# Down projection of the FFN: 14 of 22 row tiles by seven products instead of 12, one output block's plain products moved into the second phase, and ScalarE's table loaded early

## Chip, cores and metric

The kernel runs as one program on one core of a Trainium2 chip. The metric is the device time of one execution in microseconds, and lower is better. PE is TensorE, DVE is VectorE, ACT is ScalarE, SP issues the DMAs.

## What is computed

Two decoder layers run on a sequence of 512 tokens with a width of 1024. Each layer is a half-step FFN, a mixer of three branches, and a second half-step FFN, and each of these ends in a residual sum and a layer norm. So there are four FFNs, and they are what the change touches:

```
def swiglu(x, w_gate, w_up, w_down):
    return (jax.nn.silu(x @ w_gate) * (x @ w_up)) @ w_down

h = layer_norm(DEEPNORM_ALPHA * h + 0.5 * swiglu(h, ffn1_w_gate[l], ffn1_w_up[l], ffn1_w_down[l]), ln1_g[l], ln1_b[l])
mix = hybrid_mixer(h, cos, sin, ...)
h = layer_norm(DEEPNORM_ALPHA * h + mix, ln2_g[l], ln2_b[l])
h = layer_norm(DEEPNORM_ALPHA * h + 0.5 * swiglu(h, ffn2_w_gate[l], ffn2_w_up[l], ffn2_w_down[l]), ln3_g[l], ln3_b[l])
```

`x` is 512 x 1024, `w_gate` and `w_up` are 1024 x 2816, and `w_down` is 2816 x 1024. Everything is float32.

## The kernel before

**Splitting.** A float32 product is made of three fp32r matmuls (`mm3`): high by high, high by low, low by high. So each operand has to be split first. ACT casts the high part (`S.copy(h, src)`), and DVE subtracts it to get the low part (`split_into`). Every 512 columns of weight or of hidden feature thus cost one ACT and one DVE instruction before PE can use them.

**Down projection.** `token_out` computes the down product with tokens as output rows: four token tiles `tt` of 128 rows, two column halves `hf` of 512. Each (tt, hf) is one PSUM bank, and there are eight banks. The inner dimension has 22 row tiles of 128 (`NF`). The first `2 * DOWN_FAST` of them go through `seven_out`, the rest are plain products.

**Seven products.** `seven_out` takes row tile f with row tile g = f + n, and cuts the problem into a 2 x 2 block product: token halves (tiles 0 and 1, tiles 2 and 3), row tiles (f, g), column halves. It uses a seven-product scheme in place of the eight block products. Its three phases loop over all pairs: phase 1 makes two products per pair (banks `x` and `y`), phase 2 three (`v`, `x`, `y`), phase 3 two (`z`, `v`). A product is two token tiles by three matmuls of 512 columns, so 6 matmuls. Between the phases DVE adds what a bank holds so far to the residual (`norm.add`). Phase sums of operands (`t1`, `t3`, `t2`, `t4`, and those of the hidden features) are made on DVE.

**Plain row tiles.** After `seven_out`, the other row tiles are taken two at a time (a "plain pair", one weight block of 256 rows by 512 columns from `load`): first for hf 0 and all four token tiles, where `prepare` also splits the two hidden features, then for hf 1. In the second half `TAIL = 5` holds all five blocks at once, so that the token tiles end one after the other. Each is then normalised (`norm.half`, `norm.finish`), written out and transposed into the next stage's input (`to_features`).

**Order.** Nothing runs in the order written. A `Planner` records every instruction with an estimated cost, gives it a due time (PE's clock at the point where it was recorded, plus a bias), and lays all engines' queues out by a list schedule before the program is built. Buffers bound how far an engine may run ahead: 76 slots of 128 x 512 (`N_SLOTS`), of which 28 for streamed weights (`WEIGHTS`), 5 raw weight buffers (`RAWS`), 8 PSUM banks.

**Tables.** `rope_setup` runs beside the first FFN's down projection with a bias of 60 us. It uses ACT's Sin. The mixer's first special function after it is the Exp in `params`.

Of the kernel before, what the change touches and what calls it, by code (L numbers as in the profile page):

```python
# [13 lines left out]
AF = mybir.ActivationFunctionType  # L14
# [5 lines left out]
NT = T // 128  # L20
KD = D // 128
FF = 2816
NF = FF // 128
# [5 lines left out]
ALPHA = (2 * DEPTH) ** 0.25  # L29
# [265 lines left out]
FIRST_BIAS = 0.1  # L295
SECOND_BIAS = 0.6
SUM_BIAS = 6.0
TAIL = 5
DOWN_FAST = 6
TAIL_OUT = 4  # L300
WINDOW = 150.0
KEEP_LATER = 3.0
# [45 lines left out]
def trunk(tc, a, out):  # L348
    pl = Planner(tc)

    with ExitStack() as ctx:
# [12 lines left out]
        def bank(name="ps"):  # L364
            return pl.tile(ps_p, [128, 512], F32, "ps", 8)

        def small(shape, name, bufs=None):
            return pl.tile(tiny, shape, F32, name, bufs or 2)
# [177 lines left out]
                    to_features(tt, self.then == "mixer")  # L546

        LO, HI = slice(0, 256), slice(256, 512)

        def token_out(norm, wsrc, n, ah, al, tail, prepare=None, a32=None, fast=0):  # L550


            def load(hf, fp, hold=False):
                return wblock(wsrc[fp * 256:(fp + 1) * 256, hf * 512:(hf + 1) * 512], hold)

            def acc(ps, tt, f, w, j, first, more):
                c = slice(tt * 128, (tt + 1) * 128)
                mm3(ps, ah[f][:, c], al[f][:, c], w[0][j], w[1][j], first, f == n - 1, more)

            banks = seven_out(norm, wsrc, a32, fast) if fast else {}  # L560
            norm.load()
            for hf in range(2):
                ps = [banks.get((tt, hf)) or bank("dn") for tt in range(NT)]
                old = [(tt, hf) in banks for tt in range(NT)]
                rest = tail if hf else 0
                for fp in range(fast, n // 2 - rest):
                    w = load(hf, fp)
                    for j in range(2):
                        if prepare and not hf:
                            prepare(2 * fp + j)  # L570
                        for tt in range(NT):
                            acc(ps[tt], tt, 2 * fp + j, w, j, fp + j == fast and not old[tt], old[tt])
                ws = [load(hf, fp, True) for fp in range(n // 2 - rest, n // 2)]
                for tt in range(NT):
                    for i, w in enumerate(ws):
                        for j in range(2):
                            f = n - 2 * rest + 2 * i + j
                            acc(ps[tt], tt, f, w, j, f == 2 * fast and not old[tt], old[tt])
                    norm.half(tt, hf, ps[tt])
                    if hf:  # L580
                        norm.finish(tt)

        def seven_out(norm, wsrc, a32, n):
            pairs = [(i, n + i) for i in range(n)]

            def rows(f, cols=slice(0, D)):
                m = cols.stop - cols.start
                raw = pl.tile(wraw_p, [128, m], F32, "raw", RAWS)
                Q.dma_start(out=raw, in_=wsrc[f * 128:(f + 1) * 128, cols])
                return [raw[:, c:c + 512] for c in range(0, m, 512)]  # L590

            def wsplit(w):
                h, lo = slot(F32R, WEIGHTS), slot(F32R, WEIGHTS)
                split_into(h, lo, w)
                return h, lo

            def halves(op, c):
                return op[0][:, c], op[1][:, c]

            def product(to, op, w, i, more=False):  # L600
                for t in range(2):
                    c = slice(t * 128, (t + 1) * 128)
                    mm3(to[t], op[0][:, c], op[1][:, c], w[0], w[1], i == 0 and not more, i == n - 1, more)

            two = lambda: [bank("dn") for _ in range(2)]
            x, y = two(), two()
            s23, t2 = [], []
            for i, (f, g) in enumerate(pairs):
                b11, b12 = rows(f)
                s = slot()  # L610
                s23.append(s)
                V.tensor_tensor(s[:, HI], a32[f][:, LO], a32[f][:, HI], op=SUB)
                V.tensor_tensor(a32[f][:, HI], a32[f][:, HI], a32[g][:, HI], op=ADD)
                op = split(a32[f])
                t1 = slot(F32, WEIGHTS)
                V.tensor_tensor(t1, b12, b11, op=SUB)
                product(x, halves(op, LO), wsplit(b11), i)
                product(y, halves(op, HI), wsplit(t1), i)
            for t in range(2):
                norm.add(t, 0, x[t])  # L620
                norm.add(2 + t, 1, y[t])
            v = two()
            for i, (f, g) in enumerate(pairs):
                (b11, b12), (b22,) = rows(f), rows(g, slice(512, 1024))
                s = s23[i]
                V.tensor_tensor(s[:, LO], a32[f][:, HI], a32[f][:, LO], op=SUB)
                V.tensor_tensor(a32[f][:, LO], a32[g][:, LO], s[:, LO], op=SUB)
                op = split(s)
                s4 = slot(F32R)
                s4 = s4[:, LO], s4[:, HI]  # L630
                split_into(*s4, a32[f][:, LO])
                t3 = slot(F32, WEIGHTS)
                t2.append(slot())
                V.tensor_tensor(t3, b22, b12, op=SUB)
                V.tensor_tensor(t2[i], t3, b11, op=ADD)
                product(v, halves(op, HI), wsplit(t3), i)
                product(x, halves(op, LO), wsplit(t2[i]), i, True)
                product(y, s4, wsplit(b22), i, True)
            for t in range(2):
                norm.add(2 + t, 1, v[t])  # L640
                norm.add(t, 1, x[t])
                norm.add(2 + t, 0, x[t])
                norm.add(2 + t, 1, x[t])
            z = two()
            for i, (f, g) in enumerate(pairs):
                b21, = rows(g, slice(0, 512))
                op = split(a32[g])
                t4 = slot(F32, WEIGHTS)
                V.tensor_tensor(t4, b21, t2[i], op=SUB)
                product(z, halves(op, LO), wsplit(b21), i)  # L650
                product(v, halves(op, HI), wsplit(t4), i, True)
            return {(0, 0): z[0], (1, 0): z[1], (2, 0): v[0], (3, 0): v[1], (0, 1): y[0], (1, 1): y[1]}

# [89 lines left out]
        def ffn(l, wg, wu, wd, g, b, src, then, beside=None):  # L745
# [40 lines left out]
                with pl.stream(bias=60.0):  # L786
                    beside()
            residual(src)
            token_out(Norm(g[l], b[l], 4 * ALPHA, 16 * EPS, then), wd, NF, hh, hl, TAIL, prepare, hid, DOWN_FAST)


        def rope_setup():
# [22 lines left out]
            V.scalar_tensor_tensor(ang, ang, -1.0, ang, op0=MUL, op1=MAX)  # L815
            V.tensor_scalar(ang, ang, -1.0, float(np.float32(np.pi / 2)), op0=MUL, op1=ADD)
            S.activation(cos, ang, AF.Sin)
            Q.dma_start(out=trig[:, 0], in_=cos)
            Q.dma_start(out=trig[:, 1], in_=sin)

# [585 lines left out]
```

## Time and profile before

| what | value |
|---|---|
| median of 3 runs | 2413.03 us (2411.71 to 2415.16) |
| time of the profiled execution | 2411.15 us |
| its span from first to last instruction | 2409.4 us |
| granted TensorE clock over the span | 0.999 |
| busy: PE, DVE, ACT | 2384.3, 2219.6, 1332.8 us |

The profiled execution's own time is 1.75 us over its span, and 1.9 us under the median. Busy time is the union of an engine's instruction records. Matmul and vector records overlap the next one's, so the distance from start to start in a dense run tells more of the cost than a record's length does. All instructions carry line L288, which is the planner's issuing loop, so groups are told apart by tiles and shapes: `s` is any slot, `raw` a weight as it came from memory, `ps` a PSUM bank, `xh` and `xl` the split features.

### The profile page before, as it was taken

What the parts mean: (1) busy time and instruction counts of PE and PEld (TensorE: products, weight loads), DVE (VectorE), ACT (ScalarE), POOL (GpSimd) and SP (SyncE); (2) the same over time, 40 slices, a digit from 0 to 9 for tenths busy, and PEclk for the clock granted to TensorE, in tenths of its full rate; (3) what the DMA queues carried; (4) which work ended last, traced back from release to release, by engine and by line L of the source; (5) the groups of instructions that cost most, each with busy time, mean ns of one, the idle gap of its engine ahead of it and who ended that gap; (6) DMA issues with size and microseconds to landing.
All of it is one profiled execution on the core that took longest, in us unless ns stands there. A gap on an engine that the chain in (4) does not pass through costs nothing.

```text
span 2409.4 us, 41697 instructions
## 1 busy us (share of the span) xinstructions
PE 2384.3 (99%) x15812; PEld 2185.5 (91%) x15812; DVE 2219.6 (92%) x4567; ACT 1332.8 (55%) x2863; POOL 0.2 (0%) x4
## 2 busy tenths in 40 slices
PE   9999999999999999999999999999999999999998
PEld 8999888889899899998899998888889998999986
DVE  8998987999999799989799999789999997999996
ACT  6555538536756445656356565294376563555560
POOL 0000000000000000000000000000000000000000
PEclk9999999999999999999999999999999999999999
DMA  5334562322233623334523345523123335233451
GB/s 168 106 110 154 160 183 71 104 55 74 78 107 97 210 71 106 105 115 158 183 88 106 105 157 173 167 58 99 43 74 97 105 106 184 88 106 106 148 162 67
DMA packets 269834, 280.34 MB, mean 116 GB/s; under 512 B 18676, under 2 KB 221632, under 8 KB 269632
## 3 DMA queue, kind: packets, MB, share of 16 engines
q1 hardware_dynamic: 269632, 277.67, 38.3%
q8 instruction: 124, 2.03, 0.3%
q14 instruction: 78, 0.64, 0.1%
HBM read 260.33 MB, written 17.30 MB: 115 GB/s over the span
## 4 chain that ended last, share of the span: by engine, by line
PE 90%; DVE 5%; ACT 3%; DMA 1%; issue 1%; SPq 0%; DVEq 0%; ACTq 0%
PE ps L288 90%; DVE s L288 4%; ACT s L288 2%; ACT ps L288 1%; DMA raw<-in_w_out 0%; DMA raw<-in_w_in 0%; ACT xh L288 0%; DMA s<-in_x 0%; DVE lny L288 0%; DVE lnt L288 0%; DVE xl L288 0%; DMA xspill<-s 0%; DMA s<-in_cv_dw_b 0%; SPq L288 0%; DVE mx L288 0%
## 5 line engine op out<-in xcount | busy, mean ns | idle before, releaser
L288 PE MATMUL ps<-s 128*128 128x256 f32 (+2 forms) x9164 | 1516.3, 321 | 2.8 <-ACT s L288 1.9
L288 PEld LDWEIGHTS ps<-s 128*128 128x128 f32 x9164 | 1331.7, 190 | 133.6 <-ACT s L288 4.7
L288 PE MATMUL ps<-xh,s 128*128 128x256 f32 (+2 forms) x4064 | 901.4, 307 | 1.2 <-ACT s L288 1.2
L288 DVE TENSOR_TENSOR s<-s 128x512 fp32r<-128x512 f32 (+8 forms) x1264 | 718.3, 601 | 6.5 <-ACT s L288 4.2
L288 PEld LDWEIGHTS ps<-xh,s 128*128 128x128 f32 (+1 forms) x4064 | 678.7, 190 | 34.3 <-ACT s L288 1.6
L288 PE MATMUL ps<-xl,s 128*128 128x256 f32 (+2 forms) x2032 | 624.6, 308 | 0.0
L288 ACT CAST s<-raw 128x512 fp32r<-128x512 f32 (+1 forms) x716 | 424.1, 620 | 258.1 <-DMA raw<-in_ffn_w_down 67.7
L288 DVE TENSOR_TENSOR s<-raw,s 128x512 fp32r<-128x512 f32 (+1 forms) x844 | 549.3, 680 | 12.6 <-ACT s L288 10.9
L288 ACT CAST s<-s 128x512 fp32r<-128x512 f32 (+2 forms) x796 | 441.7, 591 | 165.6 <-DVE s L288 157.1
L288 ACT COPY s<-ps 128x256 f32<-128x256 f32 (+4 forms) x616 | 254.9, 419 | 349.6 <-PE ps L288 347.4
L288 PEld LDWEIGHTS ps<-xl,s 128*128 128x128 f32 (+1 forms) x2032 | 386.9, 190 | 16.7 <-DVE xl L288 0.2
L288 DVE SCALAR_TENSOR_TENSOR s<-s 128x512 f32<-128x512 f32 (+26 forms) x356 | 250.3, 714 | 2.9 <-ACT s L288 2.6
L288 DVE TENSOR_TENSOR s<-ps,s 128x256 f32<-128x256 f32 (+1 forms) x336 | 147.0, 438 | 62.8 <-PE ps L288 51.7
L288 DVE TENSOR_TENSOR s<-raw 128x512 f32<-128x512 f32 x256 | 172.9, 682 | 5.3 <-DMA raw<-in_ffn_w_gate 3.8
L288 ACT ACTIVATE s<-s 128x512 f32<-128x512 f32 x162 | 102.5, 667 | 51.5 <-DVE s L288 49.1
L288 PE MATMUL ps<-ident,s 128*128 128x128 f32 (+1 forms) x508 | 86.9, 278 | 11.8 <-DMA s<-in_x 4.5
L288 ACT CAST xh<-ps 128x512 fp32r<-128x512 f32 x48 | 28.6, 596 | 124.3 <-PE ps L288 124.3
L288 DVE TENSOR_TENSOR s<-s,raw 128x512 f32<-128x512 f32 x128 | 87.2, 681 | 0.0
L288 PEld LDWEIGHTS ps<-ident,s 128*128 128x128 f32 (+1 forms) x508 | 61.1, 142 | 28.5 <-issue 11.1
L288 DVE TENSOR_TENSOR s<-s,ps 128x512 f32<-128x512 f32 x76 | 50.5, 680 | 30.1 <-PE ps L288 30.0
L288 DVE SCALAR_TENSOR_TENSOR s<-s,ps 128x512 f32<-128x512 f32 x96 | 63.2, 679 | 15.9 <-PE ps L288 14.5
L288 DVE SCALAR_TENSOR_TENSOR s<-ps,s 128x510 f32<-128x510 f32 (+3 forms) x88 | 64.4, 740 | 0.1
(100 smaller groups left out, 573.5 us busy)
## 6 DMA issues: line engine op xcount, KB each, us to landing
raw<-in_w_in SPq DMA_DIRECT2D x106, 512.0 KB, 3.8
raw<-in_ffn_w_down SPq DMA_DIRECT2D x88, 512.0 KB, 4.4
raw<-in_ffn_w_gate SPq DMA_DIRECT2D x80, 512.0 KB, 3.8
raw<-in_ffn_w_up SPq DMA_DIRECT2D x80, 512.0 KB, 3.8
raw<-in_ffn_w_down SPq DMA_DIRECT2D x48, 256.0 KB, 2.6
spill<-s SPq DMA_DIRECT2D x40, 256.0 KB, 2.0
s<-spill SPq DMA_DIRECT2D x40, 256.0 KB, 4.2
raw<-in_w_out SPq DMA_DIRECT2D x16, 512.0 KB, 4.4
```

The costliest lines, as they stand in the source:

```text
L288: self.issued = o["f"](*o["a"], **o["k"])
```

## The change

`DOWN_FAST` goes from 6 to 7: seven pairs of row tiles go by seven products, and four plain pairs are left instead of five. In `seven_out` the roles of the two token halves are swapped (`LO`, `HI`, and the banks that go with them), so that the block which `seven_out` finishes by itself is token tiles 0 and 1 of hf 1, instead of tiles 2 and 3. For that block the plain products go to two banks of their own (`mine`), and they are made inside phase 2: `ahead()` is called after pairs 1, 2, 3, ... of phase 2 and makes one plain pair each time, with its `prepare`. After `seven_out` the plain weights of hf 0 are all held (`ws`), those of hf 1 are loaded and split a second time (`ws2`) for token tiles 2 and 3, and the token tiles end one after the other. In `rope_setup` a Tanh of one column is added behind the second Sin.

```diff
-TAIL = 5
-DOWN_FAST = 6
+AHEAD_AT = 1
+DOWN_FAST = 7
...
-            banks = seven_out(norm, wsrc, a32, fast) if fast else {}
+            banks = {}
+            if fast:
+                mine = [bank("dn") for _ in FIRST]
+                pairs = iter(range(fast, n // 2))
+
+                def ahead():
+
+                    for fp in pairs:
+                        w = load(1, fp)
+                        for j in range(2):
+                            prepare(2 * fp + j)
+                            for tt in FIRST:
+                                acc(mine[tt], tt, 2 * fp + j, w, j, fp + j == fast, False)
+                        return
+                banks = seven_out(norm, wsrc, a32, fast, ahead)
             norm.load()
+            if fast:
+                for fp in pairs:
+                    raise ValueError("pairs left")
+                ws = [load(0, fp, True) for fp in range(fast, n // 2)]
+                ws2 = []
+                for tt in range(NT):
+                    if tt in SECOND and not ws2:
+                        ws2 = [load(1, fp, True) for fp in range(fast, n // 2)]
+                    for hf, w2 in enumerate((ws, ws2)):
+                        ps = mine[tt] if hf and tt in FIRST else banks[tt, hf]
+                        if ps not in mine:
+                            for i, w in enumerate(w2):
+                                for j in range(2):
+                                    acc(ps, tt, 2 * fast + 2 * i + j, w, j, False, True)
+                        norm.half(tt, hf, ps)
+                    norm.finish(tt)
+                return
...
-        def seven_out(norm, wsrc, a32, n):
+        def seven_out(norm, wsrc, a32, n, ahead):
+            LO, HI = slice(256, 512), slice(0, 256)
...
+                if i >= n + AHEAD_AT:
+                    ahead()
             for t in range(2):
-                norm.add(t, 0, x[t])
-                norm.add(2 + t, 1, y[t])
+                norm.add(2 + t, 0, x[t])
+                norm.add(t, 1, y[t])
...
+                if i >= AHEAD_AT:
+                    ahead()
             for t in range(2):
-                norm.add(2 + t, 1, v[t])
+                norm.add(t, 1, v[t])
+                norm.add(2 + t, 1, x[t])
+                norm.add(t, 0, x[t])
                 norm.add(t, 1, x[t])
-                norm.add(2 + t, 0, x[t])
-                norm.add(2 + t, 1, x[t])
+            for _ in pairs:
+                ahead()
...
-            return {(0, 0): z[0], (1, 0): z[1], (2, 0): v[0], (3, 0): v[1], (0, 1): y[0], (1, 1): y[1]}
+            return {(2, 0): z[0], (3, 0): z[1], (0, 0): v[0], (1, 0): v[1], (2, 1): y[0], (3, 1): y[1]}
...
-            token_out(Norm(g[l], b[l], 4 * ALPHA, 16 * EPS, then), wd, NF, hh, hl, TAIL, prepare, hid, DOWN_FAST)
+            token_out(Norm(g[l], b[l], 4 * ALPHA, 16 * EPS, then), wd, NF, hh, hl, 0, prepare, hid, DOWN_FAST)
...
             S.activation(cos, ang, AF.Sin)
+
+            S.activation(small([128, 1], "one"), cos[:, 0:1], AF.Tanh)
```

## Rows read from the trace of the kernel before

**Rows 1.** The page: the span, the busy time of PE, its weight loads, DVE and ACT, and the chain of work that ended last by engine.
```profile
span 2409.4 us, 41697 instructions
PE 2384.3 (99%) x15812; PEld 2185.5 (91%) x15812; DVE 2219.6 (92%) x4567; ACT 1332.8 (55%) x2863; POOL 0.2 (0%) x4
PE 90%; DVE 5%; ACT 3%; DMA 1%; issue 1%; SPq 0%; DVEq 0%; ACTq 0%
```

**Rows 2.** The chain that ended last, in order of time (start us, us, what): a piece in the first FFN's down projection, the long pieces that hold the other three, and the pieces behind the last matmul.
```profile
272.69 10.30 DVE s L288 x17
...
864.29 349.42 PE ps L288 x2459
...
1221.62 321.37 PE ps L288 x2260
...
2058.09 342.12 PE ps L288 x2398
2400.23 0.70 DVE s L288
...
2405.65 0.66 DVEq L1402
```

**Rows 3.** Busy time of each engine in the four stretches of the down projection, from its first products to the last matmul of the plain part (stretch: us, then busy us and instructions of PE, weight loads, DVE, ACT, GpSimd, then granted clock, DMA share, GB/s).
```profile
237.50:352.60 115.10, 114.31 (x520) 94.63 (x519) 105.94 (x205) 59.43 (x108) 0.00 (x0) 1.00 0.57 170
1093.80:1208.10 114.30, 114.30 (x522) 94.88 (x521) 101.87 (x192) 57.17 (x105) 0.00 (x0) 1.00 0.49 155
1434.60:1549.00 114.40, 114.40 (x524) 95.14 (x524) 101.93 (x200) 54.90 (x103) 0.00 (x0) 1.00 0.56 165
2288.50:2400.20 111.70, 111.69 (x498) 92.20 (x496) 93.72 (x181) 43.29 (x80) 0.00 (x0) 1.00 0.37 117
```

**Rows 4.** The same columns for the stretch behind each of the first three: the start of the mixer, of the next FFN, and of the second mixer.
```profile
352.60:375.00 22.40, 20.42 (x170) 19.89 (x169) 16.34 (x43) 8.91 (x18) 0.00 (x0) 1.00 0.63 190
1208.10:1231.00 22.90, 22.77 (x187) 22.13 (x187) 22.46 (x58) 12.18 (x29) 0.00 (x0) 1.00 0.20 69
1549.00:1571.00 22.00, 21.35 (x174) 20.50 (x173) 15.65 (x39) 9.20 (x18) 0.00 (x0) 1.00 0.62 192
```

**Rows 5.** PE's timeline (start us, us, instruction, count) inside the second FFN's down projection: two unbroken runs of 512-column matmuls.
```profile
1103.69 20.56 PE L288 MATMUL ps<-s 128*128 128x512 f32 x90
...
1123.64 26.68 PE L288 MATMUL ps<-s 128*128 128x512 f32 x117
```

**Rows 6.** DVE's timeline in the same stretch: a run of twelve low-part subtractions of 512 columns, a run of one of 256 columns and one of 512, and the three longest idle times near its end (idle us and what ended it in brackets).
```profile
1160.33 7.30 DVE L288 TENSOR_TENSOR s<-raw,s 128x512 fp32r<-128x512 f32 x12
...
1119.83 1.01 DVE L288 TENSOR_TENSOR s<-s 128x256 f32<-128x256 f32 x2
...
1172.46 1.90 DVE L288 TENSOR_TENSOR s<-raw,s 128x512 fp32r<-128x512 f32 x3 [2.26 <-ACT s L288]
1177.11 1.37 DVE L288 TENSOR_TENSOR s<-s,ps 128x512 f32<-128x512 f32 x2 [2.75 <-PE ps L288]
...
1185.95 0.69 DVE L288 TENSOR_TENSOR s<-s,ps 128x512 f32<-128x512 f32 x1 [3.89 <-PE ps L288]
```

**Rows 7.** DVE's groups in that stretch by shape (count, busy us, mean ns of one record, idle before): the low parts of weights.
```profile
L288 DVE TENSOR_TENSOR s<-raw,s 128x512 fp32r<-128x512 f32 x44 | 28.5, 682 | 2.7 <-ACT s L288 2.6
```

**Rows 8.** DVE's timeline in that stretch: the eight additions of bank contents to the residual at the end of phase 2.
```profile
1132.35 1.27 DVE L288 TENSOR_TENSOR s<-s,ps 128x512 f32<-128x512 f32 x2
1133.59 1.28 DVE L288 SCALAR_TENSOR_TENSOR s<-s,ps 128x512 f32<-128x512 f32 x2
1134.79 0.68 DVE L288 TENSOR_TENSOR s<-s,ps 128x512 f32<-128x512 f32 x1
1135.39 1.28 DVE L288 SCALAR_TENSOR_TENSOR s<-s,ps 128x512 f32<-128x512 f32 x2
1136.58 0.68 DVE L288 TENSOR_TENSOR s<-s,ps 128x512 f32<-128x512 f32 x1
```

**Rows 9.** PE's timeline in the first FFN's down projection, where it waited (idle us and what ended it in brackets).
```profile
283.03 3.26 PE L288 MATMUL ps<-s 128*128 128x512 f32 x13 [0.79 <-DVE s L288]
```

**Rows 10.** PE's timeline behind the down projections of the first and the third FFN: the transposes of token tiles 2 and 3 into the mixer's input, with the wait before them.
```profile
355.31 0.63 PE L288 MATMUL ps<-ident,s 128*128 128x128 f32 x4 [1.74 <-DVE s L288]
...
362.79 0.63 PE L288 MATMUL ps<-ident,s 128*128 128x128 f32 x4 [0.24 <-DVE s L288]
...
1550.27 0.63 PE L288 MATMUL ps<-ident,s 128*128 128x128 f32 x4 [0.31 <-DVE s L288]
...
1557.74 0.63 PE L288 MATMUL ps<-ident,s 128*128 128x128 f32 x4 [0.23 <-DVE s L288]
```

**Rows 11.** DVE's timeline at the same two places: the second low part of token tile 1's features, with its wait.
```profile
349.10 0.69 DVE L288 TENSOR_TENSOR xl<-ps,xh 128x512 fp32r<-128x512 f32 x1 [1.68 <-ACT s L288]
...
1544.05 0.69 DVE L288 TENSOR_TENSOR xl<-ps,xh 128x512 fp32r<-128x512 f32 x1 [0.26 <-ACT s L288]
```

**Rows 12.** ACT's timeline: from the load of Sin's table to the work behind the second Sin, and from the cast before the next table load to the Exp behind it.
```profile
304.67 1.28 ACT L288 ACT_TABLE_LOAD   x1
...
308.75 0.63 ACT L288 ACTIVATE s<-s 128x512 f32<-128x512 f32 x1 [1.12 <-DVE s L288]
312.57 1.14 ACT L288 CAST s<-raw 128x512 fp32r<-128x512 f32 x2 [3.18 <-DMA raw<-in_ffn_w_down]
...
346.47 0.61 ACT L288 CAST xh<-ps 128x512 fp32r<-128x512 f32 x1
347.09 1.28 ACT L288 ACT_TABLE_LOAD   x1
348.39 0.20 ACT L288 ACTIVATE sc<-sc 128x4 f32<-128x4 f32 x1
```

**Rows 13.** The page's DMA issues of the down weights (count, KB each, median us to landing), and the DMA columns (last two) of two stretches near the end of the second FFN's down projection.
```profile
raw<-in_ffn_w_down SPq DMA_DIRECT2D x88, 512.0 KB, 4.4
raw<-in_ffn_w_down SPq DMA_DIRECT2D x48, 256.0 KB, 2.6
...
1150.00:1160.00 10.00, 10.00 (x46) 8.29 (x45) 10.00 (x18) 4.91 (x9) 0.00 (x0) 1.00 0.97 315
1160.00:1170.00 10.00, 10.00 (x46) 8.29 (x45) 9.52 (x16) 6.21 (x11) 0.00 (x0) 1.00 0.86 254
```

More of the change, by code (lines that the diff above doesn't have):

```diff
@@ L548, in trunk @@
         LO, HI = slice(0, 256), slice(256, 512)
+        FIRST, SECOND = (0, 1), (2, 3)
         def token_out(norm, wsrc, n, ah, al, tail, prepare=None, a32=None, fast=0):
@@ L568, in token_out @@
                     for j in range(2):
-                        if prepare and not hf:
-                            prepare(2 * fp + j)
                         for tt in range(NT):
```

## The prediction

> **What bounds the kernel now.** I read the page first. PE is busy for 2384.3 of 2409.4 us, DVE for 2219.6, and 90% of the chain that ended last is PE [rows 1]. So time is won by taking matmuls out, as long as DVE (92%) keeps up. Then the chain in order of time: the down projections of the second, third and fourth FFN lie in unbroken pieces of PE of 349, 321 and 342 us; only the first FFN's has a piece of DVE in it, 10.3 us long [rows 2]. The stretches say how much room DVE has there: it is idle for 115.1 - 105.9 = 9.2 us in the first down projection, 12.4 in the second, 12.5 in the third, 18.0 in the fourth [rows 3]. Behind the second there is next to none (22.9 - 22.46 = 0.4), in the mixers some 6 us [rows 4].
>
> **Matmuls taken out.** A seven-product pair takes 7 x 6 = 42 matmuls of 512 columns, two plain row tiles 2 x 8 x 3 = 48. One pair more saves 6 of 492 per FFN, 24 in all. In dense runs such matmuls start (20.56 - 0.39) / 89 = 0.2266 us apart, 0.39 being about the length of the last record, and the second run gives the same [rows 5]. Gain: 24 x 0.2266 = 5.44 us if PE never waits more than now. The stage goes from 111.5 to 110.1 us. Moving the plain products of one block changes no count.
>
> **Work added to DVE.** Back to back, DVE's 512-column instructions start (7.30 - 0.68) / 11 = 0.602 us apart, and a 256-column one takes 1.01 - 0.68 = 0.33 [rows 6]. By the code a pair in phase 1 needs 4 long and 2 short instructions (3.07 us, beside 2.72 of PE), in phase 2 six and three (4.60, beside 4.08), in phase 3 four (2.41, beside 2.72): 10.1 us in all. Two plain row tiles needed six (3.6 us). On top, the hf 1 weights of the four plain pairs are now split twice, which adds 4 x 2 x 0.602 = 4.8. Sum: 10.1 - 3.6 + 4.8 = +11.3 us per FFN. ACT gains less than 8 us of its own beside 50 us of idle time in the stage [rows 3], so it is costed at nothing.
>
> Does this fit? Two accounts. First the peak inside `seven_out`: DVE's work from the stage's start minus PE's. Before: 6 x 10.1 + 12 additions x 0.602 = 67.8 against 42 x 6 x 0.2266 = 57.1, so DVE must be 10.7 us ahead when the stage starts, and it is, since PE does not wait in three of the four stages [rows 2]. After: 7 x 10.1 + 7.2 + four calls of `ahead` at 2.41 = 87.5 against (294 + 48) x 0.2266 = 77.5, so 10.0 us. The moved products bring as much PE work as DVE work (12 matmuls, 2.72 us, against 2.41) and pay for the seventh pair. The test in phase 1 is never true (i stops at 6), and phase 2 has calls enough for all four pairs. So no new stall here. Then the whole stage: DVE needs 11.3 us more in 1.4 us less. That leaves 18.0 - 12.7 = 5.3 us in the fourth stage, -0.2 and -0.3 in the third and second, -3.5 in the first. The third's lack has 6 us of room behind it, the second's only 0.4 [rows 4]. The first's falls into a stretch with room, though one where PE waits on chains of DVE and ACT. I take 1 us of new PE wait for the first and 0.5 for the second: +1.5. The bounds are 0 (work of low due time slides into idle time) and +22 (each of the three tight stages can use only half of its idle time, 6 us: three times that plus what does not fit). I lean to the low end since three stages show no wait of PE today.
>
> **Banks.** Phase 2 now holds all eight banks (`x`, `y`, `v`, `mine`), so `z` has to wait until DVE has read `x`. Before, two were spare. The eight reads take 4.9 us [rows 8]. The first `z` bank needs three reads of an `x` that is complete one product (1.36 us) before the phase ends, so it is free about half a us late, and the first two `v` products of phase 3 (2.7 us) can go in between. Bounds: 0, and 4.9 - 2.7 = 2.2 us per stage. I take 0, because the list schedule may reorder and DVE has the operands early.
>
> **Memory.** Each FFN loads 4 blocks of 512 KB and 2 of 256 KB more, 2.5 MB. The end of the stage moved 250 to 315 GB/s already [rows 13]; `ws` and `ws2` together are 4 MB for 33 us, 127 GB/s, with the next stage's weights behind them on SP's queue. Hidden; if the cover is gone, one late block costs its 4.4 us. The 16 slots of `ws2` also take room from the next stage's first weights until token tile 3 has used `ws`.
>
> **The table.** Sin's table is followed today by a second load at 347.1, between two features of token tile 1, and the Exp behind it starts 1.30 us later [rows 12]. DVE waits 1.68 us there for ACT, and 0.26 in the second mixer, which needs no load [rows 11]; PE then waits 1.74 us for token tile 2 in the first, 0.31 in the second [rows 10]. So the load costs PE 1.43 us. With the Tanh it moves right behind the Sin, where ACT idles for 3.18 us until a weight lands [rows 12]: -1.43 (bounds: 0, if it lands on another wait, and -1.74). The Trainium skill, "ScalarE: Activation LUTs", What ACT_TABLE_LOAD costs, gives a drain of about 1380 ns beside the 1283 ns of the load, 2.66 us in all. By that page the sum would be 1.2 us lower; the trace does not show that drain.
>
> **The end of the stage.** Token tiles 0, 1 and 2 now end 27.2, 21.8 and 10.9 us before the last matmul (the last two take 48 matmuls each); today all four are 30 matmuls, 6.8 us, apart. Their norms no longer queue up in DVE, so what is left of the waits for tiles 2 and 3 (0.31 + 0.31 + 0.24 + 0.23 [rows 10]) should shrink: -0.6, bounds 0 and -1.1. The end of the kernel stays: DVE starts with the last matmul there and needs the same chain [rows 2]. The wait of 0.79 us in the first FFN [rows 9] comes from `rope_setup`, which still falls into phase 2 or 3; it stays.
>
> **Sum.** -5.44 - 1.43 - 0.6 + 1.5 = -6.0 us. Against the profiled execution's 2411.15 that is 2405.2; the median of the runs is 1.9 higher, so 2407.0.
>
> **Rivals.**
> - The gain is eaten: every stage loses 1.5 us of PE, to the `z` banks or to a late split. -5.44 - 2.0 + 6 = -1.4, so 2411.6. For it: eight banks of eight, and DVE without idle time. Against: PE finds other products to do.
> - DVE becomes the bound, ending slower. The place is the plain part, where `ws2` and the norms of tiles 0 and 1 fall due together. If half of the idle time is unusable, the three tight stages lose 22 us: 2413.0 - 7.5 + 22 = 2427.5. It decides for slower once new waits pass 12.3 us, some 3 to 4 per stage. For it: negative room in three stages. Against: DVE's idle times of 2.3, 2.8 and 3.9 us near the end were waits for lack of work [rows 6].
> - No overlap on DVE. Records of these instructions are 0.682 us long [rows 7], against 0.602 from start to start. If the added ones took their whole length, each FFN would gain 16 x 0.682 + 5 x 0.42 = 13.0 us of DVE, and lack 5.2, 2.0 and 1.9 us in the first three: -7.5 + 9.1 = +1.6, 2414.6. The Trainium skill, "VectorE: DVE Perf Modes", The DRAIN you can't avoid, says that the next instruction waits until the pipe is empty, and would have it so. The twelve in 7.30 us contradict it [rows 6].
> - More is won: no new wait, and the waits of rows 9 and 10 all go: -5.44 - 2.5 - 0.8 = -8.7, 2404.3 [rows 9, 10].
> - The table part does nothing, because the mixer's start waits on something else: -5.44 - 0.6 + 1.5 = -4.5, 2408.5.
>
> **How the numbers follow.** Chances: forecast 0.52 (2404 to 2409.5), gain eaten 0.22, DVE bound 0.10, more won 0.08, no table gain 0.05, no overlap 0.03. A measurement can tell 0.2%, 4.8 us, from no change, so faster means below 2408.2. Of the forecast 0.45 lies there, with 0.08 of "more" and 0.03 of "no table gain": 0.56. The rest of these (0.07 and 0.02), with 0.22 and 0.03, makes 0.34 within. Slower is 0.10. The range, 2403 to 2413.5, takes in the forecast, "more" and most of "gain eaten", and leaves out "DVE bound", "no overlap" and the edges.
>
> **What would show it.** 24 matmuls fewer; DVE busy some 45 us more; in the down stretches no wait of PE over 1 us; no table load near the first mixer's start, and the wait of 1.74 us gone. It is wrong if PE shows waits on DVE in phase 3 or the plain part, or on a bank at the start of phase 3, or if the next FFN's first products wait for their weights.

## The result, and the profile after

The changed kernel takes 2427.94 us (median of four runs, 2425.19 to 2428.19) against 2413.7 for the kernel before beside it: a ratio of 1.0059, interval 1.0047 to 1.0071. It is slower by 14.2 us where 6.0 less was forecast, and it lies outside the range. The profiled execution took 2427.96 us, 1.9 over its span.

The page of the changed kernel, answering [rows 1]: the span, busy time and instructions by engine, the bytes moved, and the chain that ended last by engine.

```profile
span 2426.1 us, 41864 instructions
PE 2391.0 (99%) x15788; PEld 2184.1 (90%) x15788; DVE 2262.0 (93%) x4651; ACT 1360.2 (56%) x2916; POOL 0.2 (0%) x4
DMA packets 274314, 290.82 MB, mean 120 GB/s; under 512 B 19060, under 2 KB 222016, under 8 KB 274112
PE 81%; DVE 10%; DMA 4%; ACT 3%; issue 1%; DVEq 0%; SPq 0%; ACTq 0%
```

The counts are as forecast: 24 matmuls fewer, and DVE busy 42.4 us more, with 84 instructions more. The chain is 81% PE where it was 90%, and DVE has 10% of it; such shares point at DVE but settle nothing, for the chain of e13 below, a kernel faster than before, has 81% and 12%.

To see where the time went I cut both traces at the first and the last 512-column matmul of the unbroken run that makes up each down projection and each mixer's output product (us, worked out from the traces, good to some 0.4; `up` is the rest of an FFN, `mix` all of a mixer ahead of its output product; the output products are alike and left out):

| | up 1 | down 1 | mix 1 | up 2 | down 2 | up 3 | down 3 | mix 2 | up 4 | down 4 |
|---|---|---|---|---|---|---|---|---|---|---|
| before | 239.2 | 113.1 | 465.0 | 228.6 | 112.0 | 229.0 | 111.8 | 462.4 | 228.6 | 110.1 |
| after | 240.8 | 123.6 | 466.1 | 228.6 | 113.0 | 228.4 | 112.6 | 462.3 | 231.5 | 109.6 |

The first down projection loses 10.5 us. The second and third lose 1.0 and 0.8 instead of gaining 1.4. Of the four only the last, with no stage behind it, gains (0.5). The two profiled spans differ by 16.7 us. What is left of that lies ahead of the first down projection (1.6), in the first mixer (1.1) and in the fourth `up` (2.9). There PE waits three times, 2.1 us together, for casts on ACT that come behind weight loads of 5.0 to 5.1 us, where the kernel before has no wait.

The busy time of the engines in the four down projections of the changed kernel, to be read beside [rows 3] (same columns):

```profile
239.10:364.60 125.50, 117.32 (x512) 94.70 (x512) 115.59 (x229) 67.35 (x125) 0.00 (x0) 0.97 0.60 179
1107.30:1222.20 114.90, 113.54 (x517) 93.53 (x516) 111.81 (x216) 63.48 (x117) 0.00 (x0) 1.00 0.56 180
1448.80:1563.30 114.50, 113.18 (x513) 93.16 (x511) 111.74 (x220) 63.63 (x120) 0.00 (x0) 1.00 0.63 193
2305.10:2416.80 111.70, 111.22 (x497) 91.76 (x496) 104.66 (x201) 51.41 (x95) 0.00 (x0) 1.00 0.44 149
```

DVE's busy time rises by 9.7 to 10.9 us in each, so its cost per FFN was sized well. In the second and third stage DVE is left with 3 us of idle time, and PE is no longer busy throughout. The chain in order of time (start us, us, what) shows what PE waited behind. In [rows 2] the second and third stage lay in one piece of PE, and the first had one piece of DVE:

```profile
296.18 11.70 DVE s L288 x21
313.22 8.18 PE ps L288 x33
322.73 9.09 DMA raw<-in_ffn_w_down
344.87 20.42 PE ps L288 x87
...
1125.94 5.90 DVE s L288 x11
...
1160.08 14.08 DVE s L288 x24
1184.27 7.61 DMA raw<-in_ffn_w_down
1204.28 28.46 PE ps L288 x174
```

In the second FFN's stage (1107 to 1222) the long pieces are now DVE's, and one is a weight that took 7.6 us to land. A landing of 9.1 us stands in the first stage too, ahead of PE's piece at 344.87.

PE's timeline in the first down projection (start us, us, instruction, count, and in brackets the wait before it), beside [rows 9]:

```profile
300.64 3.04 PE L288 MATMUL ps<-s 128*128 128x512 f32 x12 [1.93 <-DVE s L288]
304.08 3.09 PE L288 MATMUL ps<-s 128*128 128x512 f32 x12 [0.40 <-ACT s L288]
308.52 1.19 PE L288 MATMUL ps<-s 128*128 128x512 f32 x4 [1.36 <-DVE s L288]
310.35 2.11 PE L288 MATMUL ps<-s 128*128 128x512 f32 x8 [0.64 <-ACT s L288]
313.22 28.56 PE L288 MATMUL ps<-s 128*128 128x512 f32 x123 [0.76 <-DVE s L288]
344.87 1.12 PE L288 MATMUL ps<-ident,s 128*128 128x128 f32 x4 [3.09 <-DVE s L288]
...
346.92 9.28 PE L288 MATMUL ps<-s 128*128 128x512 f32 x32
```

One wait of 0.79 us has become five, 5.1 us together, at the start of phase 3, and a sixth of 3.09 us before token tile 0's transposes. Then 32 matmuls take 9.28 us where 0.2266 each would be 7.25. The windows of these 15 us say why (the columns of rows 3; the third from the right is the granted clock):

```profile
340.00:345.00 5.00, 1.91 (x9) 1.26 (x8) 5.00 (x17) 0.91 (x3) 0.00 (x0) 0.89 0.63 168
345.00:350.00 5.00, 5.00 (x16) 4.20 (x17) 4.14 (x11) 3.77 (x8) 0.00 (x0) 0.50 0.69 248
350.00:355.00 5.00, 5.00 (x22) 4.11 (x21) 3.97 (x10) 0.45 (x1) 0.00 (x0) 0.93 0.69 183
```

From 343.87, 1.0 us before the wait ended, PE was granted half its clock, 1.2 GHz, for 6.8 us. In the kernel before, this occurs only behind the last matmul. In the window that holds the wait (340 to 345) DVE was busy for all 5 us.

What DVE did at the start of phase 3, in its timeline (single lines out of a dense run):

```profile
295.24 0.42 DVE L288 CAST s<-s 128x512 f32<-128x512 int32 x1
...
297.77 0.42 DVE L288 TENSOR_SCALAR s<-s 128x512 f32<-128x512 f32 x1
...
303.23 0.69 DVE L288 SCALAR_TENSOR_TENSOR s<-s 128x512 f32<-128x512 f32 x1
```

These work on neither weights (`raw`) nor banks (`ps`): they are `rope_setup`'s reduction of angles, laid between the products' splits. Phase 3 now begins 58 us into the stage, and `rope_setup` is due after 60. Before, phase 3 had ended at 57, and the rope lay beside plain products, as DVE's timeline there shows:

```profile
295.90 0.42 DVE L288 CAST s<-s 128x512 f32<-128x512 int32 x1
```

So the rope hardly moved (its first instruction starts 56.7 us into the stage before, 54.4 now); phase 3 came to it. This also means that the wait of 0.79 us at 283.03 [rows 9] was not the rope's, as the prediction has it: the rope begins 13 us behind that wait.

In the second FFN's stage PE waits twice on DVE, at the start of phase 3 and before tile 0's transposes:

```profile
1167.42 35.66 PE L288 MATMUL ps<-s 128*128 128x512 f32 x156 [0.16 <-DVE s L288]
1204.28 0.66 PE L288 MATMUL ps<-ident,s 128*128 128x128 f32 x4 [1.20 <-DVE s L288]
```

### The profile page after: what moved, and what is told of

It is laid out like the page before. It is cut to its first block, busy times and chain, and to the rows that moved or that the text cites. A ratio compares the mean times of both kernels' runs of the same rounds, so it can differ in the third digit from the quotient of the medians.

```text
span 2426.1 us, 41864 instructions
## 1 busy us (share of the span) xinstructions
PE 2391.0 (99%) x15788; PEld 2184.1 (90%) x15788; DVE 2262.0 (93%) x4651; ACT 1360.2 (56%) x2916; POOL 0.2 (0%) x4
## 3 DMA queue, kind: packets, MB, share of 16 engines
q8 instruction: 123, 2.02, 0.3%
## 4 chain that ended last, share of the span: by engine, by line
PE 81%; DVE 10%; DMA 4%; ACT 3%; issue 1%; DVEq 0%; SPq 0%; ACTq 0%
PE ps L288 81%; DVE s L288 9%; ACT s L288 3%; DMA raw<-in_ffn_w_down 2%; DMA raw<-in_ffn_w_up 1%; DMA raw<-in_ffn_w_gate 1%; DMA raw<-in_w_in 1%; ACT ps L288 0%; DMA raw<-in_mla_w_o 0%; DVE st L288 0%; ACT xh L288 0%; DVE xl L288 0%; DMA s<-in_x 0%; DVE lny L288 0%; DVE lnt L288 0%
## 5 line engine op out<-in xcount | busy, mean ns | idle before, releaser
L288 PEld LDWEIGHTS ps<-s 128*128 128x128 f32 x9140 | 1328.6, 190 | 148.3 <-ACT s L288 10.9
L288 DVE TENSOR_TENSOR s<-s 128x512 fp32r<-128x512 f32 (+8 forms) x1304 | 746.2, 607 | 8.0 <-ACT s L288 5.4
L288 DVE TENSOR_TENSOR s<-raw,s 128x512 fp32r<-128x512 f32 (+3 forms) x876 | 574.3, 687 | 13.2 <-ACT s L288 12.5
L288 ACT CAST s<-raw 128x512 fp32r<-128x512 f32 (+1 forms) x744 | 439.6, 620 | 259.1 <-DMA raw<-in_ffn_w_down 90.5
L288 ACT CAST s<-s 128x512 fp32r<-128x512 f32 (+2 forms) x820 | 457.1, 591 | 206.2 <-DVE s L288 179.7
L288 DVE SCALAR_TENSOR_TENSOR s<-s 128x512 f32<-128x512 f32 (+27 forms) x356 | 253.0, 722 | 0.2
L288 DVE TENSOR_TENSOR s<-raw 128x512 f32<-128x512 f32 x264 | 180.9, 690 | 4.6 <-DMA raw<-in_ffn_w_gate 4.1
L288 ACT ACTIVATE s<-ps,s 128x512 f32<-128x512 f32 x58 | 40.1, 717 | 44.1 <-PE ps L288 44.0
```

What stands on the lines that cost most here:

```text
L288: self.issued = o["f"](*o["a"], **o["k"])
```

## The experiments

Two theories: the rope meets phase 3 in DVE's queue (R), or the price is the general one of seven pairs and of mixing, in every stage (G). Beside each run stands its ratio to the kernel before and the interval. "The kernel after" and "before" say from which kernel an edit starts.

**The rope moved later** (e1_rope_mixer, from after; it was meant for the mixer).

```diff
-                with pl.stream(bias=60.0):
+                with pl.stream(bias=130.0):
```

> The changed kernel with one number changed: the rope set-up beside the first FFN's down projection gets a bias of 130 us instead of 60, so it falls due about 20 us into the mixer, and no longer at the boundary of phase 2 and 3. Theory A, the set-up's DVE work collides there with seven_out's and costs the first down projection some 12 us: that stretch (240.9 to 364.4 in the changed kernel, 123.5 us) falls to 112 to 114 us, the waits of PE on DVE at 300 to 313 and at 345 go, and the time is 12 us under the changed kernel's 2427.9, about 2416. Theory B, DVE has too much work in every down projection: the stretch falls by 5 us at most, the time to about 2423. Theory C, most of the loss is a reshuffled plan of the mixers: no change in the first stretch.

Measured: 2418.06 us, 1.0022 (1.0012 to 1.0031). The first down projection falls from 123.6 to 113.8, and the kernel by 9.9 us. So R holds for 70% of the distance from before to after; 5 us over before remain.

The rope did not get as far as the mixer. Its DVE work lies from 319.58 to 357.65, most of it beside the first FFN's plain products, and another function stands between its two Sins, so ACT loads a table two more times than in after. DVE's timeline with the start of the rope, then ACT's with the second and the fourth of the four loads:

```profile
319.58 0.42 DVE L288 CAST s<-s 128x512 f32<-128x512 int32 x1
```

```profile
357.62 1.28 ACT L288 ACT_TABLE_LOAD   x1
...
363.02 1.28 ACT L288 ACT_TABLE_LOAD   x1
```

The load at 357.62 is a piece of the chain that ends at a wait of PE of 2.52 us in the first mixer (367.06). So what moving the rope won is the start of phase 3, and some of the 5 us that remain are the price of its new place. The other runs with a bias of 130 have the rope beside the plain products too, except e13.

**The rope moved earlier, ahead of the down projection** (e2_rope_up, from after): the bias is -100.

> The changed kernel with the rope set-up's bias at -100 us instead of 60, so that it falls due in the gate and up products of the first FFN, where DVE has some 10% of idle time. Theory A: about 2416, as with the set-up in the mixer, and no wait over 1 us in the first down projection but the one before the first transposes (1.2 to 1.3 us in the second and third). Theory B: 2423 or more. If the set-up costs 5 us wherever it lies: 2421.

Measured: 2419.09 us, 1.0027 (1.0016 to 1.0038). First down projection 114.6, and 1.8 us more ahead of it than in after. Either place away from phase 3 does.

**The rope's work twice** (e9_rope_twice, from after): it is also made beside the third FFN.

```diff
-                spill if l else a["x"][0], "mixer", None if l else rope_setup)
+                spill if l else a["x"][0], "mixer", rope_setup)
```

> The changed kernel with the suspected cause doubled: the rope set-up, with its bias of 60 us, runs beside the third FFN's down projection too (it writes the same tables again). If the set-up's collision is what the first down projection loses, the third one goes from 112.6 to 120 to 124 us, with PE's waits on DVE at the start of phase 3, and the time rises by 8 to 11 us over the changed kernel's 2427.9, to about 2437. If the first stage's loss is its own (the mixer's parameters, its start), the third stays under 115 us and the time under 2431.

Measured: 2433.55 us (two runs), 1.0085 (1.0065 to 1.0105). The third down projection goes from 112.6 to 120.0. PE's timeline there shows the pattern of the first stage of after, wait for wait but for the first (0.16 us, where after has 1.93):

```profile
1504.29 3.02 PE L288 MATMUL ps<-s 128*128 128x512 f32 x12 [0.16 <-DVE s L288]
1507.73 3.08 PE L288 MATMUL ps<-s 128*128 128x512 f32 x12 [0.42 <-ACT s L288]
1512.17 1.19 PE L288 MATMUL ps<-s 128*128 128x512 f32 x4 [1.36 <-DVE s L288]
1514.00 2.11 PE L288 MATMUL ps<-s 128*128 128x512 f32 x8 [0.64 <-ACT s L288]
1516.86 28.56 PE L288 MATMUL ps<-s 128*128 128x512 f32 x123 [0.76 <-DVE s L288]
1547.73 0.66 PE L288 MATMUL ps<-ident,s 128*128 128x128 f32 x4 [2.31 <-DVE s L288]
```

A stage that had no rope gets its loss together with the rope. That is R, shown from both sides. What the meeting costs is less certain: the time rises by 5.6 us over after, not by the 8 to 11 expected. The third down projection and the mixer behind it lose 7.4 and 3.8, but the first down projection, with the rope beside it as in after, takes 119.3 instead of 123.6, with 1.70 us before tile 0's transposes instead of 3.09.

**Control: the rope moved in the kernel before** (e6_before_rope): the bias is 130.

> The kernel before with the rope set-up's bias at 130 us instead of 60, a control. Its wait of 0.79 us at 283 goes, and with the set-up gone from the stage DVE has room: 2412 to 2413, 1 us under before at most. If the set-up cost before as much as it costs the changed kernel, 2404.

Measured: 2413.61 us, 1.0001 (0.9992 to 1.0011). Here the rope's place makes no difference; it costs when it falls due beside phase 3. The wait at the start of phase 3, expected to go, stays at 0.58 us (283.30), one more sign that it was not the rope's.

**Six pairs, but mixed** (e3_mix_six, from after): `DOWN_FAST` is 6.

> The changed kernel with 12 of 22 row tiles by seven products, as before: the mixing, the second split and the early table alone. It has as many matmuls as the kernel before, and 6 us more of DVE work per FFN. Theory A (the collision): the set-up still falls due in phase 3 of the first FFN (its end moves from 57 to 71 us), so 6 to 9 us are lost there, and the time is about 2420. Theory B (volume): half of the added DVE work is gone, so half of the loss, also about 2421, but spread evenly over the first three down projections, 2 to 3 us each.

Measured: 2425.87 us, 1.0055 (1.0038 to 1.0072). First down projection 120.9, second and third 114.9 and 114.8. Mixing with its second split, without the seventh pair, has nearly the whole loss: its 60 matmuls (five plain pairs) already move phase 3 to 54 us (240 matmuls at 0.2266), where the rope falls into it, and the second and third stage lose 3 us each to something that is not the rope.

**Seven pairs, not mixed** (e4_seven_only, from before): `DOWN_FAST = 7`, and `TAIL = 4`, since four plain pairs are left. Then **the same with the rope moved** (e8_seven_rope, bias 130).

> The kernel before with 14 of 22 row tiles by seven products and TAIL 4, nothing else: no mixing, no second split, no Tanh. 24 matmuls fewer (5.4 us), 6.5 us more of DVE work per FFN. If the seventh pair is sound and the mixing with its second split is what fails: 2408 to 2411. If the seventh pair itself overloads DVE (DVE must be 11.4 us ahead at the end of phase 3 instead of 10.7, with the set-up of the rope in phase 3): 2414 to 2420, with the waits in the first down projection.

> The kernel before with 14 of 22 row tiles by seven products, TAIL 4, and the rope set-up at 130 us: the seventh pair alone without the collision. If the collision was all that ate its 5.4 us (2417.4 with the set-up at 60 us): 2408 to 2410, first down projection near 112 us. If the extra DVE work itself makes PE wait in each stage: 2413 to 2416.

Measured: 2417.38 us, 1.0013 (1.0004 to 1.0022), and 2414.99, 1.0006 (0.9997 to 1.0015), which cannot be told from before. In e8 the second, third and fourth down projections take 111.3, 111.2 and 109.3, which is 0.6 to 0.8 under before instead of 1.4. The end of the kernel gives 1.2 back, and the fourth FFN's `up` another 1.8. So the seventh pair gains about half of what its matmuls say, and that goes elsewhere. The fourth `up` is longer in e8 as in after, so that part has to do with neither the rope nor the mixing.

**The table's part alone** (e5_tanh_only, from before): only the Tanh line of the diff.

> The kernel before with the Tanh behind the second Sin and nothing else. If the table load at 347 costs PE what the prediction took (1.43 us of the wait of 1.74 us before token tile 2's transposes): that wait falls to about 0.3 us, no table load lies between 340 and 350, and the time is 1.4 us under before. If the wait only moves on: no change.

Measured: 2411.74 us, 0.9993 (0.9983 to 1.0002), with before at 2413.6. ACT's timeline in after shows the second load where the Tanh put it, and PE's in e5 the wait before tile 2's transposes, which was 1.74 [rows 10]:

```profile
311.46 0.63 ACT L288 ACTIVATE s<-s 128x512 f32<-128x512 f32 x1 [1.16 <-DVE s L288]
312.11 1.28 ACT L288 ACT_TABLE_LOAD   x1
313.40 0.20 ACT L288 ACTIVATE one<-s 128x1 f32<-128x1 f32 x1
```

```profile
354.60 0.63 PE L288 MATMUL ps<-ident,s 128*128 128x128 f32 x4 [0.33 <-DVE s L288]
```

The wait lost 1.41 us, where 1.43 was forecast, and the kernel about 1.9, which the interval does not tell from nothing. None of the other runs that compute everything had a lower time.

**The second load and split taken out** (e7_single_split, from e1): the hf 1 weights that `ahead` loads are held in their slots and used again for token tiles 2 and 3.

```diff
-                        w = load(1, fp)
+                        w = load(1, fp, True)
+                        kept.append(w)
...
-                        ws2 = [load(1, fp, True) for fp in range(fast, n // 2)]
+                        ws2 = kept
```

> The changed kernel with the rope set-up at 130 us (2418.1) and one more edit: the weights that the mixed products of hf 1 load and split are held and used again, so that hf 1's weights are split once. DVE does 4.8 us less per FFN, and 2 MB less is loaded; in exchange 16 slots are held through phases 2 and 3. If the second split is what still costs PE 2 to 3 us per stage: the first three down projections fall to 111 to 112 us each and the time to about 2411. If slots are the shorter supply: 2420 or more, with waits of PE in phase 2. If what is left comes from elsewhere: 2418.

Measured: 2422.11 us, 1.0037 (1.0024 to 1.005), 4 us worse than e1. It takes 4.8 us of DVE and a burst of loads out of each FFN and gains nothing; the waits before tile 0's transposes are 2.12, 1.16 and 2.45. Whether the 16 slots held all that time cost what the loads had cost was not tried.

**Transposes of tiles 0 and 1 later in the plan** (e10_late_transposes, from e1), **and the unmixed seven pairs with all small repairs** (e12_seven_late: before, with `DOWN_FAST = 7`, `TAIL = 4`, rope moved, Tanh, late transposes).

```diff
-                transposes(ps, quarters(res.pop((tt, g))))
+                with pl.stream(bias=pl.bias + late):
+                    transposes(ps, quarters(res.pop((tt, g))))
```

> The changed kernel with the rope set-up at 130 us (2418.1), and the transposes of token tiles 0 and 1 at the end of each down projection (and of the output projection) due 12 us later in PE's queue. If the waits of 1.2 to 2.1 us before the first transposes are PE standing in a place that its plan reached too early: they go, and the first three down projections lose 1.2 to 2.1 us each, 2413 to 2414 in all. If they show that DVE is late as a whole: the wait comes back at the next transposes or at the next stage's start, and the time stays at 2417 to 2419.

> What should be the best mixture: the kernel before with 14 of 22 row tiles by seven products and TAIL 4, no mixing and no second split, the rope set-up at 130 us, the Tanh, and the late transposes. From 2415.0 (the same without Tanh and late transposes): the Tanh takes 0 to 1.4 us, the transposes 0 to 1.8. 2411.5 to 2414: at best level with the kernel before. If the seventh pair's matmuls are won as soon as nothing stands in their way: 2408.

Measured: 2421.16 us, 1.003 (1.0018 to 1.0043), and 2420.55, 1.0028 (1.0018 to 1.0037). In e10 the down projections' transposes stayed where they were (tile 0's start 96.5, 95.3 and 97.0 us into the stage, in e1 96.5, 95.0 and 96.1), so it says nothing of them. Those of the output products did move, by 19 and 7 of 192 matmuls, and the second and third `up` took 3.4 and 2.5 us longer than in e1. In e12 the transposes of the down projections moved too. The first three down projections are 2.6, 0.9 and 0.5 us shorter than in e8, and the stages behind them 3.9, 2.3 and 1.5 longer; the `up` stages behind the output products are 3.0 and 2.4 longer. So what a later place won in one stage was lost in the next. Both are misses.

**Less work for DVE, with loads, banks and second splits kept** (e13_less_dve, from e1): the weights of three of the seven products go in without their subtraction, so part of the computation is left out.

```diff
-                t1 = slot(F32, WEIGHTS)
-                V.tensor_tensor(t1, b12, b11, op=SUB)
...
-                product(y, halves(op, HI), wsplit(t1), i)
+                product(y, halves(op, HI), wsplit(b12), i)
...
-                V.tensor_tensor(t3, b22, b12, op=SUB)
-                V.tensor_tensor(t2[i], t3, b11, op=ADD)
-                product(v, halves(op, HI), wsplit(t3), i)
+                V.tensor_tensor(t2[i], b12, b11, op=ADD)
+                product(v, halves(op, HI), wsplit(b12), i)
...
-                V.tensor_tensor(t4, b21, t2[i], op=SUB)
...
-                product(v, halves(op, HI), wsplit(t4), i, True)
+                product(v, halves(op, HI), wsplit(t2[i]), i, True)
```

> The kernel after with the rope tables moved into the mixer (as in e1_rope_mixer, 2418.1 us, still 5 us over before), and three subtractions per pair of seven_out left out: b12 stands for b12 - b11 in phase 1, for b22 - b12 in phase 2, and t2 for b21 - t2 in phase 3. So part of the computation is left out. 21 instructions of 512 columns go from DVE in each FFN, 12.6 us at 0.602, a little more than the 11.3 that the change adds; matmuls, loads, splits, banks and the norms are as in e1. Theory A (what remains after the rope is DVE's demand in the down stages): the waits of e1 at the start of phase 3 and before the next stage's first transposes shrink to what before has, the second and third down stages come down to some 111 us (from 112.8 and 113.3), and the time is 2407 to 2411. Theory B (what remains is the order of the plain part: banks read late, loads bunched, transposes early in the plan): the waits stay, DVE only idles more, and the time stays at 2416 to 2419. In between, 2412 to 2415: both.

Measured: 2408.45 us, 0.9979 (0.9969 to 0.9989), 9.6 us under e1. PE's waits by what they waited for (us in total, times, longest), in after, in e1 and in e13:

```profile
PE ps L288 <- DVE s L288: 12.2, 13, 3.1
```

```profile
PE ps L288 <- DVE s L288: 11.1, 14, 2.5
```

```profile
PE ps L288 <- DVE s L288: 3.4, 7, 0.8
```

The kernel before has 5.0 us in seven such waits. The second FFN's stage in e1, by the windows' columns and then PE's timeline:

```profile
1099.00:1211.80 112.80, 111.71 (x502) 91.66 (x501) 109.91 (x212) 62.31 (x114) 0.00 (x0) 1.00 0.55 177
```

```profile
1157.50 35.69 PE L288 MATMUL ps<-s 128*128 128x512 f32 x156 [0.27 <-DVE s L288]
1194.01 0.66 PE L288 MATMUL ps<-ident,s 128*128 128x128 f32 x4 [0.82 <-DVE s L288]
```

The same in e13, where both waits are gone although loads, banks and second splits are the same:

```profile
1094.00:1206.10 112.10, 112.00 (x507) 92.41 (x506) 102.50 (x195) 65.37 (x121) 0.00 (x0) 1.00 0.57 180
```

```profile
1144.82 37.80 PE L288 MATMUL ps<-s 128*128 128x512 f32 x166
1182.45 0.60 PE L288 MATMUL ps<-ident,s 128*128 128x128 f32 x4
```

Of the 9.6 us the span shows 9.7: 7.9 less waiting of PE, and 1.8 less busy time, since the low clock that e1 still has for 3.4 us is gone too. So what remained in e1 goes when DVE has less to do in the down projection. One part of Theory A did not come: the second and third stage came down to 112.1 only, not to 111; the gain shows in the first mixer (466.2 to 462.1) and in the four down projections, by 0.7 to 1.7 each.

Three things in e13 differ from e1 beside the length of DVE's queue. The rope came to lie elsewhere (it starts at 350.17, not at 319.58, so most of it lies in the mixer, with two table loads, not four), and 5.8 of the 9.7 us lie in the first down projection and the first mixer, where that may count. The sums left out also held three slots of streamed weights per pair, and ACT can cast `b12` without waiting for DVE's subtraction. No run separates these. The other 3.9 us lie in stages that the rope is not in.

## Why the prediction was wrong, point by point

- **What bounds the kernel now** was right as far as it went: PE bound, with DVE at 92% as the condition.
- **Matmuls taken out** (-5.44): the count came as stated. What they are worth can be seen only with DVE out of the way: e13 is 5.0 us under before. If the 1.9 us of e5, which its interval does not tell from nothing, are the table's there too, some 3.1 is seen of -5.44 and the end of the stage's -0.6 together. The rest is not settled; the fourth `up` is 2.2 us longer in e13 than before.
- **Work added to DVE** is the step that failed, by its size. The work itself was counted well (+11.3 us per FFN; DVE's records grew by 9.7 to 10.9). Its price was taken as +1.5 between bounds of 0 and +22. The runs show 9.9 for the rope's place (after to e1) and 9.6 for the rest (e1 to e13, which leaves out as many DVE instructions as the change adds, 84, though not the same ones), 19.5 together: nearly the upper bound. How the 9.6 divide between DVE's queue, the rope's second move and the slots stays open. Two choices led to the low end. The peak account, 10.7 us ahead against 10.0, was taken at the end of `seven_out`. At the start of phase 3, where the waits came, the same counts give 6 x 7.67 + 7.2 - 40.8 = 12.4 before and 7 x 7.67 + 7.2 + 9.6 - 58.5 = 12.0 after, still no more. But it counted only `seven_out`'s own work, with none of the rope's, which in the first stage now falls due there and is 4 to 5 us (in e9 the second copy adds 11 instructions and 4.1 us to DVE's busy time). And "three stages show no wait of PE today" was read as slack, while the whole-stage account right beside it said that there was none (-3.5, -0.3, -0.2).
- **"It stays"**, of the 0.79 us [rows 9], is the sentence whose failure cost most. It took that wait for the rope's and said that the rope "still falls into phase 2 or 3". In the trace of the kernel before, the rope lies behind phase 3, so what the sentence priced at no change was the rope's first meeting with that phase. Phases 1 and 2 are longer by 78 matmuls (48 mixed in, 30 of the seventh pair), 17.7 us, and that moved phase 3 under a due time that is fixed at 60 us.
- **Banks** (0, bounds 0 to 2.2 per stage): a wait on DVE at the start of phase 3 shows in the first, second and fourth stage of e1, 0.53, 0.27 and 0.65 us. In e13 it is gone with the same banks, so the number of banks alone does not make it.
- **Memory** ("hidden"): wrong for the burst, as the windows at the second loads show, and ACT's timeline there:

```profile
1180.00:1190.00 10.00, 10.00 (x46) 8.26 (x45) 7.97 (x14) 3.62 (x7) 0.00 (x0) 1.00 0.97 318
```

```profile
1189.19 1.14 ACT L288 CAST s<-raw 128x512 fp32r<-128x512 f32 x2 [5.55 <-DMA raw<-in_ffn_w_down]
```

  My 127 GB/s was a mean over 33 us; in one stretch of 10 us 318 GB/s were moved, and ACT waited 5.55 us. PE ran on all the same at that time, but the chain that ends at the wait before tile 0's transposes passes through such a landing in each of the first three stages (9.09, 7.61 and 7.46 us); a piece of DVE stands right ahead of each. e13 keeps the same loads and has no such wait, so the burst alone does not make it.
- **The table** (-1.43): right on the wait, 1.41; on the kernel about 1.9, within its interval of nothing. The Trainium skill, "ScalarE: Activation LUTs", What ACT_TABLE_LOAD costs, would add a drain to the load. No such gap shows in after: the load at 312.11 begins 0.02 us behind the end of the Sin, and the next activation starts 1.29 us after it.
- **The end of the stage** (-0.6): the waits for tiles 2 and 3 went, except one of 0.31 us in the third stage. A longer one, however, stands before tile 0, 1.2 to 3.1 us in the first three stages, where DVE reaches tile 0's norm late. In e13, which takes work from DVE ahead of it, that wait is gone.
- **Rivals.** The number of "DVE becomes the bound", 2427.5, is what came, and its engine was right; that the number fits is largely chance. Its place was right only in part: it named the plain part, `ws2` and the norms, and waits did come before tile 0's transposes. But some 70% came with the rope, in one FFN's stage, and e7, which takes the second splits out of the plain part, gained nothing. Of the signs of being wrong, waits on DVE in phase 3 and in the plain part both came. Its chance of 0.10 was too low for a case with negative room in three stages.

## What to carry to other kernels

An engine that shows no waits at 92% busy is not an engine with room: sum its work against the stage that gets shorter, and take a negative sum as a price, even where today's trace is clean. When an edit lengthens one phase, list everything that is due at a fixed time or offset and ask beside what it lands now; here 11 DVE instructions, 4 to 5 us together, free where they met plain products, cost 10 us where they met phase 3. Taking work from the engine that one suspects told more in one run than moving queues about did in three. But a list schedule plans anew at every edit: look in the trace where each piece came to lie before you call the rest unchanged. The rope that e1 sent to the mixer did not get there.

## What the runs showed of the hardware

I had not expected the granted clock to fall within the body of the kernel. It fell to 0.50 for 6.8 us from within the 3.09 us wait in after, and for 3.4 us in e9 behind the 2.31 us shown above. The same is in e1, behind a wait in the first mixer (PE's timeline), and in e3, where two waits stand close together:

```profile
367.06 1.69 PE L288 MATMUL ps<-ident,s 128*128 128x128 f32 x8 [2.52 <-DVE s L288]
```

```profile
306.72 1.20 PE L288 MATMUL ps<-s 128*128 128x512 f32 x4 [1.46 <-DVE s L288]
309.83 15.39 PE L288 MATMUL ps<-s 128*128 128x512 f32 x54 [1.92 <-ACT s L288]
```

It was 3.4 us in e1 and 6.8 in e3. In after PE was at work for 5.8 of the 6.8 us, which at half the clock is a loss of 2.9 us (an estimate), so that wait cost about twice what it shows: 3.09 and 2.9.

The length of a wait does not tell by itself whether the clock falls. It fell behind 2.02 us in e2 (1539.00) and behind 2.00 and 2.45 in e7 (367.57, 1538.71), and not behind 2.08 and 1.94 in e1 (336.92, 1536.31) or 2.12 in e7 (339.13). The five waits at the start of phase 3 in after have no fall behind them; the like waits in e9's first stage have one of 3.4 us (309.80). In e4 it fell for 3.4 us at 1790.58 with no wait over 0.72 us near it.
